# Solving the last slots of a fused matmul and decayed scan in halves of time, with shared PSUM banks for their transposes

## The chip, the cores and the metric

The kernel runs on one core of a Trainium2 chip. The metric is the time of one execution on the device in microseconds (us), the median of three timed runs. A profile of one further execution gives the span from its first to its last instruction, and each engine's instructions within it. TensorE is called PE, VectorE DVE, ScalarE ACT, GpSimd POOL, and SP is the engine that issues the stores.

## The reference

```python
B, S, D = (16, 2048, 1024)
xw = x @ w                       # x: B x S x D, w: D x D
out[:, 0, :] = xw[:, 0, :]
for t in range(1, S):
    out[:, t, :] = decay[None, :] * out[:, t - 1, :] + xw[:, t, :]
```

Each of the 1024 output channels is a first-order recurrence over time, run separately in each of 16 batches. All arrays are float32.

## The kernel before

**Tiling.** The 16 x 2048 time steps are cut into 64 chunks of 512. Input is loaded as bfloat16 with time on the partitions, transposed on DVE and copied by ACT into tiles `xt`, which hold input channels on the partitions and time along the free axis. The output channels are cut into K = 8 groups `n` of 128. A slot is one group of chunks (two chunks, or one chunk in the last two) with one `n`. For a slot, PE sums eight matmuls of 128 x 128 weights per chunk in a PSUM bank of 512 float32 columns: 128 output channels on the partitions, time along the free axis.

**Recurrence.** DVE runs it along the free axis with one scan instruction, in one of two ways. In an unpaired slot one scan (`run`, line 233) reads the PSUM bank and writes the solved tile `so`. In a paired slot ACT copies the bank to `xs` (`copy`, line 186) and scales its even columns (`odd`, line 169), POOL adds them to the odd columns (`join`, line 208), DVE scans half as many columns with the squared decay (`scan`, line 213), and then ACT scales (`even`) and POOL adds (`fill`, line 260) to recover the even columns. A tile takes the last column of the chunk before it as initial value.

**Output.** For almost all slots DVE transposes `so` in blocks of 32 x 32 into a tile `ot` (line 272), and SP stores it when four slots have filled it (line 296). The last four slots, called -4 to -1 here (R = 4; groups n = 4 to 7 of the last chunk), go another way: PE transposes each 128 x 128 block of `so` into PSUM against an identity matrix (line 398, `cross`), a copy brings the blocks of the four slots for the same 128 time steps to SBUF (line 416, `leave`), and SP stores them as 128 rows of 512 float32, which is 256 KB (line 418). The index `i` from 0 to 3 names the block of 128 time steps, and `r` from 0 to 3 names the slot: r = 0 is slot -4, r = 3 is slot -1.

**Order.** The order of instructions on each engine is that of the program. It is written by hand for the first and last slots, in the table `agenda`: a letter is an operation, the number after it the slot. `S` scans, `a` and `b` scan the first and second half of time, `h` and `c` complete a paired slot (ACT, then POOL), `R` and `V` are the functions `wedge` and `ending`. The last lines are:

```python
-3: "p-4 A-6 g-4 A-5 Z-7 Z-6 Z-5 j-4",
-2: "S-3 S-4",
-1: "a-2 h-4 c-4 a-1 R b-2 b-1 V",
```

Slot -4 is paired; slots -3, -2 and -1 are not. The matmuls of a slot are issued before its line of the table is performed. Slots -4, -3 and -2 are matmuls of 512 columns. Slot -1 alone is in halves of 256 columns, each half in a bank of its own (lines 625 to 633): eight matmuls of half 0, the transposes of slot -3 for blocks 0 and 1, six matmuls of half 1, then in `wedge` three transposes of block 0 and the last two matmuls. In `ending` the copy and store of block 0 come first, then three transposes of block 1, its copy and store, six transposes of blocks 2 and 3, and the last two (slot -1's) once its second half is scanned. Each of the four blocks has a PSUM bank and an SBUF tile of its own. ACT copies blocks 0 to 2, DVE copies block 3.

**PSUM.** There are eight banks: a ring `ps` of three tiles with room for two banks each, and one bank each named `spare` and `spare1`. `spare1` holds the squared decay, which paired scans read, until slot -4 has been scanned.

Of the kernel before, what the change touches and what calls it, by code (L numbers as in the profile page):

```python
# [14 lines left out]
def _ap(ap_obj: bass.AP, new_ap, extra_offset=0):  # L15
    return dataclasses.replace(
        ap_obj,
        ap=[list(p) for p in new_ap],
        offset=ap_obj.offset + extra_offset,
    )  # L20
# [5 lines left out]
def kernel(  # L26
# [26 lines left out]
    nc = tc.nc  # L53
    pin = tc.keep_in_program_order
    B, S, D = x.shape
    assert w.shape == (D, D)

    NQ = 4
    P = 32
    CQ = D // NQ  # L60
    K = CQ // P
    M = K // 2
    TL = 512
    NJ = TL // P
    NC = S // TL
    R = K // 2
    CH = D // 2
# [3 lines left out]
    sb = ctx.enter_context(tc.tile_pool(name="sb", bufs=1))  # L71
    psp = ctx.enter_context(tc.tile_pool(name="psp", bufs=1, space=bass.MemoryType.PSUM))
# [3 lines left out]
    def ring(pool, name, count, shape, dtype=FP32):  # L76
        i = turns[name] = turns.get(name, -1) + 1
        return pool.tile(shape, dtype, name=f"{name}{i % count}")
# [4 lines left out]
    chunks = [(b, c * TL) for b in range(B) for c in range(NC)]  # L83
    nch = len(chunks)
# [14 lines left out]
    xt_of = {}  # L99
# [25 lines left out]
    def matmul(ps, n, k, xt, t0=0, t1=TL, start=0, pairs=None):  # L125
        if pairs is None:
            rhs = xt[:, k // 2, k % 2, t0:t1]
        else:
            rhs = pairs[:, k // 2, t0 // P:t1 // P, :, k % 2].rearrange("p j i -> p (j i)")
        lhs = wsb[:, k, n].rearrange("p q i -> p (q i)")  # L130
        pin(nc.tensor.matmul(  # L131
            out=ps[:, t0:t1] if ps.shape[1] >= t1 else ps,
            lhsT=lhs,
            rhs=rhs,
            start=(k == 0 and t0 == start),
            stop=(k == K - 1),
        ))
# [3 lines left out]
    class Tile:  # L141
# [39 lines left out]
        def copy(self):  # L181
            self.xs = sb.tile([128, 2 * TL], FP32, name=f"xs{self.lot % 3}")[:, 0:self.T]
            parts = self.ps if isinstance(self.ps, tuple) else (self.ps,)
            size = self.T // len(parts)
            for i, ps in enumerate(parts):
                pin(nc.scalar.copy(out=self.xs[:, i * size:(i + 1) * size], in_=ps))  # L186
# [55 lines left out]
        def scan_half(self, half):  # L242
# [2 lines left out]
            ps = self.ps[half] if isinstance(self.ps, tuple) else self.ps[:, t:t + size]  # L245
            self.run(ps, t, size)

        def complete(self):
            if self.paired:
                self.even()  # L250
                self.fill()
            if self.keep is not None:
                self.save()
# [51 lines left out]
    size = M * CH  # L305
# [18 lines left out]
    spare = ring(psp, "spare", 1, [128, TL])  # L324
# [18 lines left out]
    for q in range(NQ):  # L343
        pin(nc.sync.dma_start(
            out=rows[q * P:q * P + R],
# [40 lines left out]
            out=ident, in_=ident, compare_op=ALU.not_equal, fill=1.0, base=0,  # L386
            pattern=[[-1, 128]], channel_multiplier=1))

    blocks = []

    def bank(name, count):
        return ring(psp, name, count, [128, R, 128])

    def cross(rs, some):
        for i in some:
            for r in rs:
                t = 2 + i * 128
                pin(nc.tensor.transpose(  # L398
                    out=blocks[i][:, r], in_=tiles[len(slots) - R + r].so[:, t:t + 128], identity=ident))

    def advance(count):
        for half, k, t in ends[:count]:
            matmul(half, K - 1, k, xt_of[nch - 1], t, t + TL // 2, t)
        del ends[:count]

    def wedge(i):
        cross((2, R - 1, 0), (0,))
        advance(2)

    def ending(i):  # L410
        b, t0 = chunks[-1]
        wides = [ring(sb, *spot, [128, NQ, R, P])
                 for spot in (("xb", 3), ("xb", 3), ("xb", 3), ("h", 4))]

        def leave(i, copy):
            pin(copy(out=wides[i].rearrange("p q r i -> p r q i"),  # L416
                     in_=blocks[i].rearrange("p r (q i) -> p r q i", q=NQ)))
            pin(nc.sync.dma_start(
                out=_ap(out, [[D, 128], [1, CH]], (b * S + t0 + i * 128) * D + CH),
                in_=wides[i].rearrange("p q r i -> p (q r i)")))  # L420

        leave(0, nc.scalar.copy)
        cross((2, 0, R - 1), (1,))
        leave(1, nc.scalar.copy)
        blocks.extend(bank(name, count) for name, count in (("ps", 3), ("spare", 1)))
        cross((1, 0, 2), (2, 3))
        cross((R - 1,), (2, 3))
        leave(2, nc.scalar.copy)
        leave(3, nc.vector.tensor_copy)

    slots = [(g, n) for g in groups[:-1] for n in range(K)]
    slots += [([c], n) for c in groups[-1] for n in range(K)]
    tiles = []

    def turn_and_load(c):
# [24 lines left out]
        "d": square_again,  # L460
        "I": identity,
        "V": ending,
        "R": wedge,
        "p": lambda s: tiles[s % len(slots)].copy(),
        "g": lambda s: tiles[s % len(slots)].odd(),
        "z": lambda s: tiles[s % len(slots)].zero(),
# [66 lines left out]
    }  # L533
    flips = (1, 13, 15, -19, -18, -11, -8, -6, -3, -2)
    later = {}
# [35 lines left out]
    for step, (g, n) in enumerate(slots):  # L571
        T = TL * len(g)
        left = step - len(slots)
        if n % R == 0:
            ns, nj = range(n, n + R), T // P
            if left == -2 * R:
                outlets = [Outlet(ns, H, half) for half in range(2)]
            else:
                pieces = 1 if left < -7 * R else 2 if left < -6 * R else nj // H
                outlets = [Outlet(ns, nj, pieces=pieces)]  # L580
        if left == -R:
            outlets = []
        if step == 0:
            heads = [ring(psp, "ps", 3, [128, T]) for _ in range(3)]
            firsts = [ps[:, 0:TL] for ps in heads] + [spares[0]]
            seconds = [ps[:, TL:T] for ps in heads] + [spares[1]]
            for j0, j1 in halves:
                for k in range(0, K, 2):
                    for i in range(R):
                        matmul(firsts[i], i, k, xt_of[0], j0 * P, j1 * P, pairs=xw_of[0])  # L590
            for k in range(1, K, 2):
                for i in range(R):
                    matmul(firsts[i], i, k, xt_of[0])
            for k0 in range(0, K, 2):
                for i in range(R):
                    for k in (k0, k0 + 1):
                        matmul(seconds[i], i, k, xt_of[1], 0, H * P,
                               pairs=xw_of[1] if k0 < 4 else None)
            for i in range(R):
                for k in range(K):  # L600
                    matmul(seconds[i], i, k, xt_of[1], H * P, TL, H * P,
                           pairs=xw_of[1] if i < 2 else None)
        if step < R:
            ps = heads[n] if n < 3 else tuple(spares)
        else:
            if step == K + 1:
                ps = nexts
            elif len(g) == 2 or n % R < 3:
                ps = ring(psp, "ps", 3, [128, T])
            else:  # L610
                ps = ring(psp, "spare", 1, [128, TL])
            todo = [(k, l) for k in range(K) for l in range(len(g))]
            if step < K:
                todo.sort(key=lambda kl: kl[0] % 2)
            elif step == K:
                todo = []
                nexts = (ring(psp, "spare", 1, [128, TL]), ring(psp, "ps", 3, [128, TL]))
                for l in range(len(g)):
                    for i, half in enumerate((ps[:, l * TL:(l + 1) * TL], nexts[l])):
                        for k in range(K):  # L620
                            matmul(half, n + i, k, xt_of.get(g[l]),
                                   pairs=xw_of[g[l]] if g[l] in (3,) else None)
            elif step == K + 1:
                todo = []
            if left == -1:
                ps = tuple(both[:, t:t + TL // 2] for t, both in zip(
                    (0, TL // 2), (ps, ring(psp, "ps", 3, [128, TL]))))
                blocks += [bank("spare1", 1), bank("ps", 3)]
                ends = [(half, k, t) for t, half in zip((0, TL // 2), ps) for k in range(K)]
                advance(K)  # L630
                cross((1,), (0, 1))
                advance(K - 2)
                todo = []
            if 40 <= step < 190:
                pin(nc.tensor.nop(hint="x", nofuse=True))
            for k, l in todo:
                matmul(ps[:, l * TL:(l + 1) * TL], n, k, xt_of[g[l]])
        tiles.append(Tile(g, n, ps, outlets))
        do = agenda.get(step, agenda.get(left) if left >= -20 else None)
        if do is None:  # L640
            do = usual(step)
        else:
            do = do.split()
            if left == -20:
                do = rest(step) + do
        perform(do)
# [29 lines left out]
```

## Time and profile before

| what | value |
|---|---|
| median of three timed runs | 904.1 us (904.0, 904.1, 904.33) |
| span of the profiled execution | 902.5 us |
| median less that span | 1.6 us |
| mean granted PE clock | 0.999 |
| instructions | 12285 |
| first matmul of slot -4 | 889.40 |
| matmuls of slot -1, first half | 894.58 to 895.62 |
| last matmul | ends 897.11 |
| last PE transpose | ends 898.39 |
| last copy | ends 899.12 |
| four last stores issued | 897.54, 898.09, 898.93, 899.36 |
| data of these stores on the DMA engines | 898.40 to 901.13 |

The lower rows are from the timeline of the profiled execution, in us from the span's start. A matmul's row covers its fill and drain, so the rows of neighbouring matmuls overlap; the distance of their starts is what each costs in a stream. A row such as `L131 PE MATMUL ps<-xt,wsb 128*128 128x512 bf16 x24` gives line, engine, operation, output and inputs, shapes, and how many neighbours were merged into it. At its end, in brackets, stands the idle time of the engine before it and what ended it.

### The profile page before, as it was taken

What the parts mean: (1) busy time and instruction counts of PE and PEld (TensorE: products, weight loads), DVE (VectorE), ACT (ScalarE), POOL (GpSimd) and SP (SyncE); (2) the same over time, 40 slices, a digit from 0 to 9 for tenths busy, and PEclk for the clock granted to TensorE, in tenths of its full rate; (3) what the DMA queues carried; (4) which work ended last, traced back from release to release, by engine and by line L of the source; (5) the groups of instructions that cost most, each with busy time, mean ns of one, the idle gap of its engine ahead of it and who ended that gap; (6) DMA issues with size and microseconds to landing.
All of it is one profiled execution on the core that took longest, in us unless ns stands there. A gap on an engine that the chain in (4) does not pass through costs nothing.

```text
span 902.5 us, 12285 instructions
## 1 busy us (share of the span) xinstructions
PE 896.7 (99%) x4201; PEld 411.4 (46%) x4201; DVE 824.2 (91%) x632; ACT 686.9 (76%) x958; POOL 656.6 (73%) x755
## 2 busy tenths in 40 slices
PE   9999999999999999999999999999999999999998
PEld 5544444444444444444444444444444444444444
DVE  4999998998999999999998999999999999999998
ACT  4889867777877877878778778777787787787743
POOL 7888678777767768777677687777777776876632
PEclk9999999999999999999999999999999999999999
DMA  9999999999999999999999999999999999999858
GB/s 193 194 215 220 231 231 206 215 231 243 251 249 248 242 251 246 244 250 253 227 236 228 221 228 230 232 227 227 232 230 228 227 234 223 228 226 218 183 142 236
DMA packets 403182, 204.77 MB, mean 227 GB/s; under 512 B 9392, under 2 KB 402096, under 8 KB 403120
## 3 DMA queue, kind: packets, MB, share of 16 engines
q1 hardware_dynamic: 265808, 134.77, 60.8%
q0 software_dynamic: 137024, 68.70, 56.8%
q8 instruction: 33, 0.54, 0.2%
q10 hardware_dynamic: 288, 0.52, 0.2%
q14 instruction: 29, 0.24, 0.1%
HBM read 138.42 MB, written 134.22 MB: 302 GB/s over the span
## 4 chain that ended last, share of the span: by engine, by line
PE 98%; DMA 1%; POOL 0%; issue 0%; DVE 0%; DVEq 0%; POOLq 0%
PE ps L131 96%; PE spare L131 1%; DMA xb<-in_x_dram 1%; DMA ot<-in_w_dram 1%; POOL ot L313 0%; PE spare L398 0%; PE ps L398 0%; DVE h L416 0%; DVE wsb L320 0%; DVEq L320 0%; POOLq L660 0%
## 5 line engine op out<-in xcount | busy, mean ns | idle before, releaser
L131 PE MATMUL ps<-xt,wsb 128*128 128x512 bf16 x4016 | 866.1, 378 | 0.5 <-DVE wsb L320 0.5
L131 PEld LDWEIGHTS <-wsb 128*128 128x128 bf16 x4152 | 405.9, 98 | 479.7 <-ACT wsb L320 0.8
L208 POOL TENSOR_TENSOR xs<-h,xs 128x512 f32<-128x512 f32 (+1 forms) x190 | 242.5, 1276 | 187.1 <-ACT h L169 85.5
L186 ACT COPY xs<-ps 128x1024 f32<-128x1024 f32 (+1 forms) x190 | 188.9, 994 | 152.8 <-PE ps L131 147.7
L272 DVE STREAM_TRANSPOSE ot<-so 128x1024 f32<-128x1024 f32 (+2 forms) x264 | 300.1, 1175 | 4.5 <-DMA out_dram<-ot 2.3
L260 POOL TENSOR_TENSOR so<-h,xs 128x512 f32<-128x512 f32 (+1 forms) x190 | 241.1, 1271 | 45.2 <-ACT h L169 28.0
L123 ACT COPY xt<-xw 128x2048 bf16<-128x2048 bf16 (+1 forms) x136 | 242.2, 1789 | 7.8 <-DVE xw L115 7.8
L105 POOL DMA_DIRECT2D xb<-in_x_dram x264 | 174.0, 660 | 3.5 <-DMA ot<-in_w_dram 1.1
L169 ACT ACTIVATE h<-so,dec 128x512 f32<-128x512 f32 (+1 forms) x190 | 145.4, 766 | 29.8 <-DVE so L213 26.7
L115 DVE STREAM_TRANSPOSE xw<-xb 128x2048 f32<-128x2048 f32 (+1 forms) x78 | 147.3, 1900 | 7.0 <-DMA xb<-in_x_dram 7.0
L213 DVE TENSOR_TENSOR_SCAN so<-spare,keep,xs 128x512 f32<-128x512 f32 (+1 forms) x97 | 119.8, 1237 | 25.7 <-POOL xs L208 25.4
L213 DVE TENSOR_TENSOR_SCAN so<-spare,xs 128x512 f32<-128x512 f32 x93 | 113.1, 1218 | 26.5 <-POOL xs L208 23.6
L169 ACT ACTIVATE h<-ps,dec 128x512 f32<-128x512 f32 (+1 forms) x189 | 129.4, 685 | 0.0
L233 DVE TENSOR_TENSOR_SCAN so<-dec,ps 128x1024 f32<-128x1024 f32 x34 | 76.7, 2259 | 1.0 <-ACT h L169 1.0
L233 DVE TENSOR_TENSOR_SCAN so<-dec,keep,ps 128x1024 f32<-128x1024 f32 (+2 forms) x35 | 75.4, 2153 | 0.0
L264 ACT COPY keep<-so 128x1 f32<-128x1 f32 x136 | 25.2, 188 | 9.4 <-DVE so L233 9.0
L204 ACT COPY so<-keep 128x1 f32<-128x1 f32 x97 | 18.5, 192 | 2.7 <-DVE ot L272 2.5
L131 PE MATMUL spare<-xt,wsb 128*128 128x512 bf16 (+1 forms) x56 | 11.9, 341 | 0.0
L131 PE MATMUL ps<-xw,wsb 128*128 128x256 bf16 (+1 forms) x68 | 11.2, 301 | 0.0
L202 POOL MEMSET so<- 128x1 f32 x93 | 10.6, 116 | 0.6 <-DVE ot L272 0.6
L313 POOL DMA_DIRECT2D ot<-in_w_dram x12 | 6.5, 544 | 3.2 <-DMA xb<-in_x_dram 2.1
L338 PE MATMUL spare<-idle 128*128 128x512 bf16 x22 | 7.5, 519 | 1.2 <-DVE idle L328 1.2
(39 smaller groups left out, 39.3 us busy)
## 6 DMA issues: line engine op xcount, KB each, us to landing
out_dram<-ot SPq DMA_DIRECT2D x236, 512.0 KB, 10.9
xb<-in_x_dram POOLq DMA_DIRECT2D x248, 256.0 KB, 7.9
out_dram<-ot SPq DMA_DIRECT2D x56, 128.0 KB, 2.6
xb<-in_x_dram POOLq DMA_DIRECT2D x16, 128.0 KB, 5.8
out_dram<-ot SPq DMA_DIRECT2D x8, 256.0 KB, 4.2
ot<-in_w_dram POOLq DMA_DIRECT2D x12, 128.0 KB, 5.1
out_dram<-xb SPq DMA_DIRECT2D x3, 256.0 KB
ot<-in_w_dram ACTq DMA_DIRECT2D x2, 256.0 KB, 5.1
```

What stands on the lines that cost most here:

```text
L105: pin(nc.gpsimd.dma_start(out=xb_of[c][quad(q), j0:j1], in_=_ap(x, [[D, P], [P * D, j1 - j0], [1, CQ]], (b * S + t0 + j0 * P) * D + q * CQ)))
L115: pin(nc.vector.transpose(out=dst.rearrange("p (m j i) -> p j m i", m=M, i=P)[:, j0:j1, m0:m1], in_=src.rearrange("p (j m c) -> p j m c", ...
L123: pin(copy(out=xt_of[c][:, m0:m1, :, j0 * P:j1 * P], in_=src))
L131: pin(nc.tensor.matmul(out=ps[:, t0:t1] if ps.shape[1] >= t1 else ps, lhsT=lhs, rhs=rhs, start=(k == 0 and t0 == start), stop=(k == K - 1),))
L169: pin(nc.scalar.activation(out=h, in_=src, func=mybir.ActivationFunctionType.Copy, scale=dec[:, self.n:self.n + 1]))
L186: pin(nc.scalar.copy(out=self.xs[:, i * size:(i + 1) * size], in_=ps))
L208: pin(nc.gpsimd.tensor_tensor(out=odds, in0=self.g, in1=odds, op=ALU.add))
L213: pin(nc.vector.tensor_tensor_scan(out=so[:, 3:T + 2:2], data0=squares[-1][:, n:n + 1].to_broadcast([128, T // 2]), data1=self.xs[:, 1:T:2 ...
L233: pin(nc.vector.tensor_tensor_scan(out=so[:, t + 2:t + 2 + size], data0=dec[:, n:n + 1].to_broadcast([128, size]), data1=ps, initial=befor ...
L260: pin(nc.gpsimd.tensor_tensor(out=self.so[:, 2:T + 2:2], in0=self.h, in1=self.xs[:, 0:T:2], op=ALU.add))
L264: pin(nc.scalar.copy(out=self.keep, in_=self.so[:, self.T + 1:self.T + 2]))
L272: pin(nc.vector.transpose(out=outlet.ot[:, :, c0:c0 + P], in_=self.so[:, 2 + t0:2 + t0 + nj * P].rearrange("p (i t) -> p i t", t=P)))
```

## The change

The change touches only the last four slots and the functions that write them out.

Slot -2's matmuls are split into halves of 256 columns like those of slot -1. PE now issues: slots -4 and -3 whole, half 0 of -2, half 0 of -1, half 1 of -2, eight transposes (blocks 0 and 1 of all four slots), half 1 of -1, eight transposes (blocks 2 and 3). Slot -3's matmuls stay whole, but its scan is split into halves (`a-3`, `b-3`). Slot -4's scan moves ahead of that of slot -3. The second half of the last scan goes in two pieces of 128 columns (`e-1`, `f-1`).

The tiles of the ring `ps` for slots -4 to -2 take two banks each (`tops`). The transposes go into four banks by pairs of blocks and pairs of slots: blocks 0 and 1 of slots -4 and -3 share one bank, blocks 0 and 1 of slots -2 and -1 the next, and blocks 2 and 3 likewise share the two banks in which the matmuls of slots -4 and -3 had been. Slot -2's halves lie in the two banks of the third tile; slot -1's halves lie in `spare` and `spare1`.

The copies go piece by piece (`carry`): ACT copies 512, 256 and 256 columns for blocks 0 and 1; then ACT copies 512 columns (slots -4 and -3 of blocks 2 and 3), DVE copies 256 (slots -2 and -1 of block 2), and ACT copies twice 128 (slot -2, then slot -1, of block 3). All blocks go through one SBUF tile. The four stores stay as they were, of 256 KB each from SP.

```diff
+        def scan_part(self, t, size):
+            half = self.T // 2
+            ps = self.ps[t // half] if isinstance(self.ps, tuple) else self.ps
+            t0 = t % half if isinstance(self.ps, tuple) else t
+            self.run(ps[:, t0:t0 + size], t, size)
...
     def cross(rs, some):
-        for i in some:
-            for r in rs:
+        for r in rs:
+            for i in some:
                 t = 2 + i * 128
                 pin(nc.tensor.transpose(
-                    out=blocks[i][:, r], in_=tiles[len(slots) - R + r].so[:, t:t + 128], identity=ident))
...
+                    out=banks[i // 2 * 2 + r // 2][:, i % 2, :, r % 2],
+                    in_=tiles[len(slots) - R + r].so[:, t:t + 128], identity=ident))
+
+    def carry(copy, i0, i1, r0, r1):
+        src = banks[i0 // 2 * 2 + r0 // 2][:, i0 % 2:i0 % 2 + i1 - i0, :, r0 % 2:r0 % 2 + r1 - r0]
+        dst = wides[0][:, i0:i1, :, r0:r1]
...
+    def half_slot(s, half):
+        tile_ = tiles[s % len(slots)]
+        t = half * TL // 2
+        for k in range(K):
+            matmul(tile_.ps[half], tile_.n, k, xt_of[nch - 1], t, t + TL // 2, t)
 
     def ending(i):
...
+        wides.append(ring(sb, "xb", 3, [128, NQ, NQ, R, P]))
+        cross((1, 0, 2, 3), (0, 1))
+        half_slot(-1, 1)
+        carry(nc.scalar.copy, 0, 2, 0, 2)
+        carry(nc.scalar.copy, 0, 1, 2, 4)
+        leave(nc.sync, 0)
+        carry(nc.scalar.copy, 1, 2, 2, 4)
+        leave(nc.sync, 1)
+
+    def closing(i):
+        cross((0, 1, 2), (2, 3))
+        cross((3,), (2,))
+        cross((3,), (3,))
+        carry(nc.scalar.copy, 2, 4, 0, 2)
+        carry(nc.vector.tensor_copy, 2, 3, 2, 4)
+        leave(nc.sync, 2)
+        carry(nc.scalar.copy, 3, 4, 2, 3)
+        carry(nc.scalar.copy, 3, 4, 3, 4)
+        leave(nc.sync, 3)
...
+        "e": lambda s: tiles[s % len(slots)].scan_part(TL // 2, TL // 4),
+        "f": lambda s: tiles[s % len(slots)].scan_part(TL * 3 // 4, TL // 4),
...
-        -2: "S-3 S-4",
-        -1: "a-2 h-4 c-4 a-1 R b-2 b-1 V",
+        -2: "S-4 a-3 h-4 c-4 a-2",
+        -1: "a-1 V b-3 b-2 e-1 f-1 R",
...
+            elif -R <= left < -1:
+                tops.append(ring(psp, "ps", 3, [128, 2 * TL]))
+                ps = tops[-1][:, 0:TL]
+                if left == -2:
+                    ps = (tops[-1][:, 0:TL // 2], tops[-1][:, TL:TL * 3 // 2])
...
+        if left >= -2:
+            half_slot(left, 0)
+        if left == -1:
+            half_slot(-2, 1)
+            banks += [both[:, t:t + TL].rearrange("p (b q r i) -> p b q r i", b=2, q=NQ, r=2)
+                      for t, both in ((TL, tops[0]), (TL, tops[1]), (0, tops[0]), (0, tops[1]))]
```

More of the change, by code (lines that the diff above doesn't have):

```diff
@@ L387, in identity @@
             pattern=[[-1, 128]], channel_multiplier=1))
-    blocks = []
-    def bank(name, count):
-        return ring(psp, name, count, [128, R, 128])
+    tops = []
+    banks = []
+    wides = []
     def cross(rs, some):
-        for i in some:
-            for r in rs:
+        for r in rs:
+            for i in some:
                 t = 2 + i * 128
                 pin(nc.tensor.transpose(
-                    out=blocks[i][:, r], in_=tiles[len(slots) - R + r].so[:, t:t + 128], identity=ident))
@@ L401, in advance @@
[L401 to L408, printed above, removed]
-    def ending(i):
[L411 to L429, printed above, removed]
+                    out=banks[i // 2 * 2 + r // 2][:, i % 2, :, r % 2],
@@ new lines, in cross @@
+                    in_=tiles[len(slots) - R + r].so[:, t:t + 128], identity=ident))
+    def carry(copy, i0, i1, r0, r1):
+        src = banks[i0 // 2 * 2 + r0 // 2][:, i0 % 2:i0 % 2 + i1 - i0, :, r0 % 2:r0 % 2 + r1 - r0]
+        dst = wides[0][:, i0:i1, :, r0:r1]
+        if r1 - r0 == 2:
+            pin(copy(out=dst.rearrange("p b q r i -> p b q (r i)"),
+                     in_=src.rearrange("p b q r i -> p b q (r i)")))
+        else:
+            pin(copy(out=dst[:, :, :, 0], in_=src[:, :, :, 0]))
@@ new lines, in leave @@
+    def leave(queue, i):
+        b, t0 = chunks[-1]
+        pin(queue.dma_start(
+            out=_ap(out, [[D, 128], [1, CH]], (b * S + t0 + i * 128) * D + CH),
+            in_=wides[0][:, i].rearrange("p q r i -> p (q r i)")))
+    def half_slot(s, half):
[3 more added lines that the diff above has]
+            matmul(tile_.ps[half], tile_.n, k, xt_of[nch - 1], t, t + TL // 2, t)
+    def ending(i):
+        wides.append(ring(sb, "xb", 3, [128, NQ, NQ, R, P]))
[6 more added lines that the diff above has]
+        leave(nc.sync, 1)
@@ L462 @@
         "V": ending,
-        "R": wedge,
+        "R": closing,
+        "e": lambda s: tiles[s % len(slots)].scan_part(TL // 2, TL // 4),
+        "f": lambda s: tiles[s % len(slots)].scan_part(TL * 3 // 4, TL // 4),
         "p": lambda s: tiles[s % len(slots)].copy(),
@@ L607 @@
                 ps = nexts
+            elif -R <= left < -1:
[3 more added lines that the diff above has]
+                    ps = (tops[-1][:, 0:TL // 2], tops[-1][:, TL:TL * 3 // 2])
             elif len(g) == 2 or n % R < 3:
                 ps = ring(psp, "ps", 3, [128, T])
+            elif left == -1:
+                ps = (ring(psp, "spare", 1, [128, TL])[:, 0:TL // 2],
+                      ring(psp, "spare1", 1, [128, TL])[:, 0:TL // 2])
             else:
@@ L624 @@
                 todo = []
[L625 to L632, printed above, removed]
+            if left >= -2:
                 todo = []
@@ L638 @@
         tiles.append(Tile(g, n, ps, outlets))
+        if left >= -2:
+            half_slot(left, 0)
[3 more added lines that the diff above has]
+                      for t, both in ((TL, tops[0]), (TL, tops[1]), (0, tops[0]), (0, tops[1]))]
         do = agenda.get(step, agenda.get(left) if left >= -20 else None)
```

## The prediction

> **What bounds the kernel now.** I read the engines' busy shares first, then the chain of work that ended last, then the last 12 us in order of time, and last the DMA share in short stretches.
>
> ```profile
> PE 896.7 (99%) x4201; PEld 411.4 (46%) x4201; DVE 824.2 (91%) x632; ACT 686.9 (76%) x958; POOL 656.6 (73%) x755
> ...
> PE 98%; DMA 1%; POOL 0%; issue 0%; DVE 0%; DVEq 0%; POOLq 0%
> ```
>
> TensorE (PE) is busy for 99% of the span, and 98% of the chain is PE. The diff leaves every slot up to -4 as it is and issues the same columns of matmul (a slot of 512 becomes two halves), so about 889 us of the span can't move. What can move is what lies behind the matmuls of slot -4.
>
> ```profile
> 889.40 5.34 PE L131 MATMUL ps<-xt,wsb 128*128 128x512 bf16 x24
> ...
> 892.43 0.73 POOL L208 TENSOR_TENSOR xs<-h,xs 128x256 f32<-128x256 f32 x1 [2.19 <-ACT h L169]
> 893.11 1.28 DVE L233 TENSOR_TENSOR_SCAN so<-dec,keep,ps 128x512 f32<-128x512 f32 x1
> 894.30 0.73 DVE L213 TENSOR_TENSOR_SCAN so<-spare,keep,xs 128x256 f32<-128x256 f32 x1
> 894.58 1.04 PE L131 MATMUL spare<-xt,wsb 128*128 128x256 bf16 x8
> ...
> 896.32 1.58 DVE L233 TENSOR_TENSOR_SCAN so<-dec,so,ps 128x256 f32<-128x256 f32 x2
> ...
> 896.73 0.38 PE L131 MATMUL ps<-xt,wsb 128*128 128x256 bf16 x2
> ...
> 898.12 0.27 PE L398 MATMUL spare<-ident,so 128*128 128x128 f32 x1
> ...
> 898.43 0.69 DVE L416 COPY h<-spare 128x512 f32<-128x512 f32 x1 [0.53 <-PE spare L398]
> 899.36 0.40 SPq L418 DMA_DIRECT2D out_dram<-h  x1
> ```
>
> The columns are start, duration, engine, line and operation. Slots -4 to -2 are the 24 matmuls from 889.40 (0.216 us each). Slot -1 is in halves (0.109 each); its last matmul ends at 897.11. The last scan b-1 starts 0.06 later, the last transpose ends at 898.39, the last copy at 899.12. Four stores of 256 KB are issued at 897.54, 898.09, 898.93 and 899.36. The stretches show what ends last:
>
> ```profile
> 897.90:898.40 0.50, 0.49 (x4) 0.20 (x2) 0.00 (x0) 0.24 (x2) 0.00 (x0) 1.00 0.02 5
> 898.40:899.09 0.69, 0.00 (x0) 0.00 (x0) 0.66 (x1) 0.50 (x1) 0.00 (x0) 1.00 1.02 380
> 899.09:899.78 0.69, 0.00 (x0) 0.00 (x0) 0.03 (x1) 0.00 (x0) 0.00 (x0) 1.00 1.00 365
> 899.78:900.47 0.69, 0.00 (x0) 0.00 (x0) 0.00 (x0) 0.00 (x0) 0.00 (x0) 1.00 1.03 380
> 900.47:901.13 0.66, 0.00 (x0) 0.00 (x0) 0.00 (x0) 0.00 (x0) 0.00 (x0) 0.64 1.04 400
> 901.30:902.50 1.20, 0.00 (x0) 0.00 (x0) 0.00 (x0) 0.00 (x0) 0.00 (x0) 0.50 0.00 0
> ```
>
> The last two columns are the DMA engines' share and GB/s. The older stores are through by 897.9; from 898.40 the four stores fill all 16 engines, 0.69 us each, with no gap. So **the end is bound by the stores' data**: first packet 0.86 us behind the first issue (897.54 to 898.40), four times 0.69, and about 1.3 us of closing. The third store could start at 898.93 + 0.86 = 899.79, just when the second is through: issue and data are level there.
>
> **The change, part by part.** Times are on this execution's clock; its span is 902.5, the median of the three timed runs 904.1, so 1.6 us lie around the span and I carry them over.
>
> *DVE order.* S-4 moves ahead of slot -3's scan. It waits for the POOL add that ends at 893.16, so it starts at 893.2 instead of 894.30. The 512 scan becomes two of 256: a 256 follows the next after 0.66 (894.30 to 894.95), so two take 1.32 against 1.19 (893.11 to 894.30), +0.13. Then a-3 starts at 893.86, a-2 at 894.51, a-1 at 895.17 (ends 895.90), b-3 at 895.83, b-2 at 896.49 (ends 897.22). The matmuls each needs are done before.
>
> *Pair completion.* In the trace h-4 (ACT) starts 0.03 behind S-4's end and c-4 (POOL) ends 1.34 behind h-4's start (895.06 to 896.40). So c-4 ends near 895.3 instead of 896.40.
>
> *PE order.* Halves -2a, -1a, -2b take 3 x 0.87 from 892.85 to 895.45, then eight transposes of 0.11 to 896.33, then half -1b to 897.20, with its last matmul ending at 897.36. The transposes find a-3, c-4 (needed at 895.67, cover 0.37), a-2 and a-1 (needed at 896.11, cover 0.2) done; without that cover each microsecond of lateness costs one, because half -1b is queued behind them. Before, five transposes stood ahead of that end; now eight do: **the last matmul ends 0.25 later**.
>
> *Last scan in two.* No row shows a 128 scan. 512 takes 1.255, 256 takes 0.73; the line gives 0.46, the next start 0.40 on. Bounds are 0.17 (the DVE's 128x8 copy) and 0.73; I take the line, since 256 is near. e-1 runs from 897.42 to 897.88, f-1 from 897.82 to 898.28. The last transpose then starts at 898.33 and ends at 898.60, 0.21 later than before. The split wins nothing for that one (unsplit, the scan would end at 898.15 and the two transposes at 898.58); it only brings block 2's transpose forward, to 897.93.
>
> *First two stores.* Bank pair 0 is complete at 896.05, pair 1 at 896.49. An ACT copy of 512 takes 0.585; 256 I take at 0.37 (bounds 0.19, the one-element copy, and 0.585; the 0.48 of the strided activation lies between). The copies end near 897.0 and 897.35; the stores go out at 897.03 and 897.46 (SP's issues follow at 0.43: 898.93 to 899.36), about 0.5 and 0.6 earlier. First packet 897.93, where the older stores end; both are through at 899.31.
>
> *Last two stores.* Row blocks 2 and 3 of slots -2 and -1 now share one PSUM bank, and the DVE copy of block 2 stands in program order behind the transpose that writes block 3 there. No row of before has one engine reading a bank that PE still writes: there each bank is handed on whole (transposes end 896.89, copy starts 896.93). I take it that this stays so, and the copy waits for the last transpose: 898.64. A DVE copy of 512 takes 0.69; 256 I take at 0.42 (bounds 0.17 and 0.69). It ends at 899.06, the store goes out at 899.09 instead of 898.93, its first packet comes at 899.95. The DMA engines have then been idle since 899.31. The last two ACT copies (128 elements, 0.27 each by the same line, bounds 0.19 and 0.585) run beside or, if ACT must also wait for DVE on the bank, behind it and end at 899.1 or 899.6; the last store goes out by 899.6, ready at 900.46, before the third is through at 900.64. The end of data is 899.95 + 0.69 + 0.66 = 901.30 against 901.13.
>
> **Sum: +0.17 us**, span 902.7, time 904.3. The 0.5 us gained at the first two stores is not on the path any more: the queue runs dry and the third store sets the end. The other edits (8 more weight loads of about 0.1 beside matmuls of 0.109, as in half -1a now; no ring slot reused early; the earlier stores' issues untouched) cost nothing in this cover; if the loads were not hidden, 0.1 us each would be late.
>
> The Trainium skill, page "PSUM — Partial Sum Buffer", section "PSUM bank collisions raise a hardware error", says that two engines may not use one bank and quadrant at once, whatever the columns, so accesses need guarding by bank. That speaks against copying a shared bank piecewise, and by it the sum is the +0.17; the trace of before can't show it, as it has no such pair of accesses. The page "DMA: Bandwidth & Descriptors", section "Latency and other measured facts", gives about 0.6 us to the first byte of a store issued from SP. The 0.86 here differs from it, and the measurement decides; by 0.6 the third store would start at 899.69 and the sum would be -0.09.
>
> **The rivals.**
> 1. *The pieces do run early.* The DVE copy waits only for its own transpose (starts at 897.93, ends at 898.2) and for f-1 on its queue: it runs from 898.3 to 898.72, store three at 898.75, packets from 899.61; the last ACT copy runs from 898.64 to 898.91, store four at 899.18 (SP's 0.43), and its data ends at 900.99. That is -0.14: 904.0. For it: one SBUF tile is read in pieces by ACT (10.20) while DVE still writes other pieces (to 11.14). Against: no such row in PSUM.
> 2. *Slower: the two-bank tiles are waited for whole.* Slot -2's halves now lie in two banks of one tile. If the matmuls of -2b must wait for a-2, which reads the other half (ends 895.23), PE starts them 0.69 late; and if b-3 waits for the transposes into its tile's other bank (then ending near 897.2), b-2, e-1 and f-1 follow in line: f-1 ends at 899.4, the DVE copy at 900.2, store three has packets at 901.1 and the data ends at 902.45, +1.3: 905.4. It decides as soon as a wait covers more than a bank. Against it stand the SBUF rows of rival 1; no row of before shows it in PSUM.
> 3. *Slower: the shared output tile.* All four blocks now go through one SBUF tile. If each copy waited for the store of the block before to land (897.54 to about 899.6, 2.05 us, at the first store now), store two would go out at 899.4, three at 902.1, four at 904.6, and the data would end near 906.2: +5, 909. Before, each block had its own tile. Against: the pieces of xw above, written and read side by side.
> 4. *The order does not hold:* c-4 or a-1 is late at the transposes. Covers are 0.37 and 0.2; beyond them the price is one to one. Being 0.5 late gives 904.6.
>
> **How the numbers follow.** Forecast (shared bank waited for) 0.64, 904.3; rival 1 0.22, 904.0; rival 4 0.06, 904.6; rival 2 0.05, 905.4; rival 3 0.03, 909. The bounds on the unshown sizes move the forecast: a 128 scan as short as 0.17 makes the end of data 0.36 earlier (903.9), one as long as 0.73 makes it 0.5 later (904.8); the copy's bounds add about 0.25 either way. The range is 903.7 to 904.9. A measurement of this kernel tells about 0.2% (1.8 us) from no change; within it lie all cases but rival 3 and accidents of the kind of rivals 2 and 4. So faster 0.02, within 0.93, slower 0.05.
>
> **What would show it.** In the changed kernel: S-4 at 893.2; eight transposes in a row from 895.45 with no gap; the last matmul ending near 897.36; two scans of 0.46; the first store issued near 897.0; a gap of some 0.6 us in the DMA share near 899.3 to 899.95; the DVE copy starting behind the last transpose. I am wrong if that copy starts before it, if the DMA gap is missing, or if PE idles ahead of -2b or -1b.

## The result and the profile after

The changed kernel takes 906.39 us (8 runs, 906.15 to 906.78) where the kernel before takes 904.22 (8 runs beside it): the ratio is 1.0025, with a 95% interval of 1.0016 to 1.0034. It is slower by about 2.2 us, outside the range of 903.7 to 904.9. The profiled execution has a span of 904.8 us against 902.5. Its page, as the one of before was read, with busy time by engine and then the chain that ended last:

```profile
PE 892.1 (99%) x4127; PEld 411.9 (46%) x4209; DVE 824.9 (91%) x634; ACT 687.2 (76%) x961; POOL 656.7 (73%) x755
...
PE 97%; DMA 1%; issue 1%; DVE 0%; POOL 0%; ACT 0%; ACTq 0%; DVEq 0%; POOLq 0%
```

(Some of PE's records are missing in this trace: 4127 matmuls against 4209 weight loads.) The shares hardly move; the loss is a quarter of a per cent and lies in the last 10 us. Slot -4's first matmul starts at 889.46 here and at 889.40 before, so nothing ahead of it has changed. From there the timeline reads (start, duration, engine, line, operation; in brackets the idle time before and what ended it):

```profile
893.25 0.75 DVE L213 TENSOR_TENSOR_SCAN so<-spare,keep,xs 128x256 f32<-128x256 f32 x1
...
895.20 0.73 DVE L233 TENSOR_TENSOR_SCAN so<-dec,keep,spare 128x256 f32<-128x256 f32 x1
895.34 1.03 PE L131 MATMUL ps<-xt,wsb 128*128 128x256 bf16 x8 [0.52 <-DVE so L233]
896.21 1.04 PE L403 MATMUL ps<-ident,so 128*128 128x128 f32 x8
896.84 1.14 ACT L411 COPY xb<-ps 128x512 f32<-128x512 f32 x3 [2.27 <-PE ps L403]
897.08 1.04 PE L131 MATMUL spare<-xt,wsb 128*128 128x256 bf16 x8
897.73 4.28 SPq L418 DMA_DIRECT2D out_dram<-xb  x4
...
898.01 1.39 DVE L233 TENSOR_TENSOR_SCAN so<-dec,so,ps 128x256 f32<-128x256 f32 x2 [2.09 <-ACT xb L411]
...
899.31 0.97 DVE L233 TENSOR_TENSOR_SCAN so<-dec,so,spare 128x128 f32<-128x128 f32 x2
...
900.71 0.42 DVE L411 COPY xb<-ps 128x256 f32<-128x256 f32 x1 [0.42 <-PE ps L403]
901.17 0.43 ACT L414 COPY xb<-ps 128x128 f32<-128x128 f32 x2 [1.29 <-DVE xb L411]
```

Four waits are new. PE stands idle for 0.52 us ahead of the second half of slot -2 (-2b), until the scan a-2 has ended. DVE stands idle for 2.09 us behind a-1, until ACT's three copies of blocks 0 and 1 end at 897.98; then b-3 starts at once. The DVE copy of block 2 starts behind the last transpose (900.34 plus 0.33). And ACT's last copies start only when that DVE copy has ended. The last two waits are between users of one bank, and the forecast had them; the first two are between users of different banks of one tile, and it did not. The stretches of the DMA engines' data (last two columns: share, GB/s):

```profile
897.73:898.58 0.85, 0.60 (x6) 0.35 (x3) 0.57 (x1) 0.25 (x1) 0.00 (x0) 1.00 0.00 0
898.58:899.28 0.70, 0.44 (x2) 0.20 (x2) 0.70 (x2) 0.00 (x0) 0.00 (x0) 1.00 1.01 375
899.28:900.10 0.82, 0.55 (x3) 0.35 (x3) 0.78 (x3) 0.58 (x1) 0.00 (x0) 1.00 0.86 320
900.10:902.02 1.92, 0.39 (x2) 0.14 (x1) 0.61 (x2) 0.43 (x2) 0.00 (x0) 0.88 0.00 0
902.02:902.72 0.70, 0.00 (x0) 0.00 (x0) 0.00 (x0) 0.00 (x0) 0.00 (x0) 0.50 0.99 369
902.72:903.54 0.82, 0.00 (x0) 0.00 (x0) 0.00 (x0) 0.00 (x0) 0.00 (x0) 0.50 0.88 325
```

The first two stores are through at 900.10. The third is issued only at 901.20 and has its first packet at 902.02, so the queue is empty for 1.9 us; before, the four stores followed one another without a gap. SP's row of that third store:

```profile
901.20 0.33 SPq L418 DMA_DIRECT2D out_dram<-xb  x1
```

### The profile page after: what moved, and what is told of

It is laid out like the page before. It is cut to its first block, busy times and chain, and to the rows that moved or that the text cites. A ratio compares the mean times of both kernels' runs of the same rounds, so it can differ in the third digit from the quotient of the medians.

```text
span 904.8 us, 12223 instructions
## 1 busy us (share of the span) xinstructions
PE 892.1 (99%) x4127; PEld 411.9 (46%) x4209; DVE 824.9 (91%) x634; ACT 687.2 (76%) x961; POOL 656.7 (73%) x755
## 4 chain that ended last, share of the span: by engine, by line
PE 97%; DMA 1%; issue 1%; DVE 0%; POOL 0%; ACT 0%; ACTq 0%; DVEq 0%; POOLq 0%
PE ps L131 95%; PE spare L131 1%; DMA xb<-in_x_dram 1%; DMA ot<-in_w_dram 1%; DVE so L233 0%; POOL ot L319 0%; PE ps L403 0%; POOL xs L208 0%; ACT xb L411 0%; ACT xs L186 0%; DVE xb L411 0%; ACT h L169 0%; DVE wsb L326 0%; ACT xb L414 0%; ACTq L698 0%
```

## The experiments

**Theory T:** a tile in PSUM is waited for whole. An instruction waits for what another engine did earlier in program order on any part of the same tile, in another bank too, and also where both only read. **Rival B:** waits go by bank, as the forecast had it; then b-3's wait must come from something else (two engines reading PSUM at once, a late input), and the idle PE from the halves themselves.

Starts of the runs differ by up to a microsecond, so beside each time stands the *tail*: from the start of slot -4's first matmul to the end of the span of the profiled execution. It is 13.12 before (902.52 less 889.40) and 15.34 after (904.80 less 889.46).

| kernel | time, us | ratio to before, 95% interval | tail, us |
|---|---|---|---|
| before | 904.22 | 1 | 13.12 |
| after | 906.39 | 1.0025 (1.0016 to 1.0034) | 15.34 |
| 1: scans first | 905.27 | 1.0014 (1.0005 to 1.0023) | 14.32 |
| 2: slot -2 whole | 905.88 | 1.0021 (1.0012 to 1.0030) | 15.01 |
| 3: banks swapped | 906.03 | 1.0021 (1.0012 to 1.0030) | 14.79 |
| 4: before, one tile | 904.95 | 1.0009 (1.0000 to 1.0018) | 14.00 |
| 5: tiles apart | 904.32 | 1.0000 (0.9991 to 1.0009) | 13.04 |
| 6: apart, by block | 904.40 | 1.0001 (0.9992 to 1.0010) | 13.18 |
| 7: before, two readers | 904.52 | 1.0002 (0.9993 to 1.0011) | 13.28 |

The kernel before took 904.06 beside 1 to 4 and 904.36 beside 5 to 7. The intervals are about 0.8 us to either side. So the times tell the changed kernel and experiments 1 to 3 from the kernel before (experiment 4 barely), but not 1 to 3 from the changed kernel; what is said of those rests on the rows and the tail, from one profiled execution each.

### 1. The scans ahead of the transposes

```diff
-        -1: "a-1 V b-3 b-2 e-1 f-1 R",
+        -1: "a-1 b-3 b-2 V e-1 f-1 R",
```

> Edit: in the changed kernel the scans b-3 and b-2 stand ahead of the first eight transposes and their copies in program order; the order on each engine stays the same. Theory T (a PSUM tile is waited for whole: an instruction waits for what any other engine did earlier in program order on any part of the tile, the reads of it too): b-3 no longer comes after ACT's reads of its tile, so it follows a-1 directly at about 895.9 instead of 898.01, b-2 follows at 896.5, e-1 at about 898.2 behind the last matmul; the third store goes out near 899.9 instead of 901.16. Span 1.3 us less than the changed kernel, time about 905.1. Rival B (waits go by bank, and b-3 stands still because ACT and DVE read PSUM at the same time, or because DVE lacked something else that came late): b-3 still starts near 898.0, time 906.4.

The order on each engine is the same as in the changed kernel; only which instruction counts as earlier differs. The timeline of this kernel (slot -4 starts at 889.17):

```profile
894.92 0.72 DVE L233 TENSOR_TENSOR_SCAN so<-dec,keep,spare 128x256 f32<-128x256 f32 x1
895.05 1.03 PE L131 MATMUL ps<-xt,wsb 128*128 128x256 bf16 x8 [0.52 <-DVE so L233]
895.56 1.36 DVE L233 TENSOR_TENSOR_SCAN so<-dec,so,ps 128x256 f32<-128x256 f32 x2
895.92 1.07 PE L403 MATMUL ps<-ident,so 128*128 128x128 f32 x8
896.56 1.14 ACT L411 COPY xb<-ps 128x512 f32<-128x512 f32 x3 [2.27 <-PE ps L403]
```

b-3 now starts at 895.56, 0.64 behind a-1's start and with no idle time, and the tail is 1.02 us shorter. So b-3's 2.09 us were no lack of data. ACT's copies run from 896.56 with b-2 (until 896.92) on DVE beside them, so the wait was not for two engines reading PSUM at once either. This is as T has it. The gain is 0.3 less than expected, about half of it because e-1 and f-1 take 0.99 together and not 0.86.

### 2. Slot -2 whole

```diff
-                if left == -2:
-                    ps = (tops[-1][:, 0:TL // 2], tops[-1][:, TL:TL * 3 // 2])
...
-        if left >= -2:
-            half_slot(left, 0)
-        if left == -1:
-            half_slot(-2, 1)
+        if left == -1:
+            half_slot(-1, 0)
```

> Edit: slot -2's matmuls are whole again (eight of 512 columns into one bank of its own tile), all else of the change stays. Theory T: the idle time of 0.52 us on PE ahead of the second half of slot -2 goes, since no second half has to wait for a-2, which reads the other bank of that tile; but a-1 is then the last to be ready for the transposes (about 896.4), so half 1 of slot -1 starts only 0.36 earlier, the copies end about 0.3 earlier, and b-3, still waiting for them, starts near 897.7. Span 0.3 less than the changed kernel, time about 906.1. Rival B (the idle time is the price of having the halves at all, and b-3 waits for something else): PE has no such idle time, but b-3 does not move with the copies: time 906.4.

The timeline (slot -4 starts at 889.11):

```profile
896.17 0.44 PE L403 MATMUL ps<-ident,so 128*128 128x128 f32 x2 [0.18 <-DVE so L233]
...
896.65 0.65 ACT L411 COPY xb<-ps 128x256 f32<-128x256 f32 x2 [0.26 <-PE ps L403]
...
897.33 1.38 DVE L233 TENSOR_TENSOR_SCAN so<-dec,so,ps 128x256 f32<-128x256 f32 x2 [1.21 <-ACT xb L411]
```

The idle time ahead of -2b is gone; PE waits 0.18 for a-1 instead. The copies end at 897.30 and b-3 starts 0.03 later: it moves with them. The tail is 0.33 shorter, as T expected (0.3).

### 3. The two banks of blocks 0 and 1 swapped

```diff
-                      for t, both in ((TL, tops[0]), (TL, tops[1]), (0, tops[0]), (0, tops[1]))]
+                      for t, both in ((TL, tops[1]), (TL, tops[0]), (0, tops[0]), (0, tops[1]))]
```

> Edit: the two banks for the transposes of blocks 0 and 1 change places: those of slots -4 and -3 go into the second bank of slot -3's tile, those of slots -2 and -1 into the second bank of slot -4's tile. Nothing else changes; every bank is used as before. Theory T: b-3 reads slot -3's tile, in which ACT now reads only its first copy, which ends near 897.42; so b-3 starts near 897.46 instead of 898.01, everything behind it 0.55 earlier: span 904.2, time 905.85. Rival B (waits by bank, b-3 held by the ACT copies as such or by something else): b-3 stays at 898.0, time 906.4.

The two banks change places with all their users. The bank that b-3 reads keeps its own; only its neighbour in the tile is another. The timeline (slot -4 starts at 889.06):

```profile
896.45 1.14 ACT L411 COPY xb<-ps 128x512 f32<-128x512 f32 x3 [2.27 <-PE ps L403]
896.69 1.04 PE L131 MATMUL spare<-xt,wsb 128*128 128x256 bf16 x8
897.07 1.38 DVE L233 TENSOR_TENSOR_SCAN so<-dec,so,ps 128x256 f32<-128x256 f32 x2 [1.54 <-ACT xb L411]
```

b-3 starts at 897.07, 0.03 after the end of the first copy (896.45, and 0.59 for its 512 columns), while ACT goes on with the other two until 897.59. So it waits for the one copy that reads its own tile, and not for ACT as such. The tail is 0.55 shorter, the number expected. This run speaks most plainly against B.

### 4. The kernel before with one tile for both halves of slot -1

```diff
-                ps = tuple(both[:, t:t + TL // 2] for t, both in zip(
-                    (0, TL // 2), (ps, ring(psp, "ps", 3, [128, TL]))))
+                both = ring(psp, "ps", 3, [128, 2 * TL])
+                ps = (both[:, 0:TL // 2], both[:, TL:TL * 3 // 2])
```

> Edit: the kernel before, with one thing changed: the two halves of slot -1 lie in the two banks of one PSUM tile instead of in banks of two tiles. Theory T: a-1 waits for the six matmuls of the second half that stand ahead of it in program order, though they write the other bank: it starts near 896.5 instead of 895.65; the transpose of slot -1, the last two matmuls and b-2, b-1 behind them follow 0.7 to 0.8 late. Time about 905.0. Rival B (waits by bank): nothing changes, a-1 at 895.65, time 904.2.

The timeline (slot -4 starts at 889.14), with a-1 of the kernel before (slot -4 at 889.40) first:

```profile
895.65 0.75 DVE L233 TENSOR_TENSOR_SCAN so<-dec,keep,spare 128x256 f32<-128x256 f32 x1
...
895.42 0.82 PE L131 MATMUL ps<-xt,wsb 128*128 128x256 bf16 x6
...
896.27 0.75 DVE L233 TENSOR_TENSOR_SCAN so<-dec,keep,ps 128x256 f32<-128x256 f32 x1 [0.86 <-PE ps L131]
896.93 1.58 DVE L233 TENSOR_TENSOR_SCAN so<-dec,so,ps 128x256 f32<-128x256 f32 x2
897.08 0.44 PE L398 MATMUL spare<-ident,so 128*128 128x128 f32 x2 [0.73 <-DVE so L233]
```

a-1 reads one bank and waits 0.86 us for six matmuls that write the other. One part of the change, sharing a tile, put alone into the kernel before, costs 0.88 us of tail.

### 5. The changed schedule with the tiles apart

```diff
                 if left == -2:
-                    ps = (tops[-1][:, 0:TL // 2], tops[-1][:, TL:TL * 3 // 2])
+                    ps = (tops[-1][:, 0:TL // 2],
+                          ring(psp, "spare1", 1, [128, TL])[:, 0:TL // 2])
...
-                      ring(psp, "spare1", 1, [128, TL])[:, 0:TL // 2])
+                      tops[2][:, TL:TL * 3 // 2])
...
     def closing(i):
+        low = ring(psp, "spare", 1, [128, TL])
+        late = ring(psp, "spare1", 1, [128, TL])
+        banks.extend((view(low, 0), view(tops[1], 0), view(low, 0), view(late, 0)))
...
+            banks += [view(tops[0], TL), view(tops[0], 0)] * 2
```

Here `banks` holds two entries for each block, one for slots -4 and -3 and one for slots -2 and -1, and `view` gives one bank of a tile in the layout of the transposes.

> Edit: the changed kernel with its schedule, its halves, pieces, copies and stores as they are, and only the places in PSUM changed, so that no instruction touches a tile on which another engine still has something to do: slot -2's halves lie in two tiles, the transposes of blocks 0 and 1 all go into slot -4's tile, those of block 2 and of block 3 of slots -2 and -1 go into two tiles. Theory T: no idle time on PE ahead of slot -2's second half, b-3 right behind a-1, the DVE copy of block 2 right behind the last scan, the third store near 898.9 when slot -4 starts at 889.40 as in the kernel before; all of the 2.2 us comes back: time 904.1, span 902.5. Rival (the halves, the split scans and the smaller pieces cost time by themselves, beyond the waits): the waits go but 0.7 us or more stays, time 904.9 or above.

The timeline (slot -4 starts at 889.35):

```profile
893.68 1.91 PE L131 MATMUL spare<-xt,wsb 128*128 128x256 bf16 x16
...
895.43 1.04 PE L409 MATMUL ps<-ident,so 128*128 128x128 f32 x8
895.74 0.72 DVE L233 TENSOR_TENSOR_SCAN so<-dec,so,ps 128x256 f32<-128x256 f32 x1
896.30 1.04 PE L131 MATMUL ps<-xt,wsb 128*128 128x256 bf16 x8
896.38 0.72 DVE L233 TENSOR_TENSOR_SCAN so<-dec,so,spare 128x256 f32<-128x256 f32 x1
896.50 1.14 ACT L417 COPY xb<-ps 128x512 f32<-128x512 f32 x3 [2.04 <-PE ps L409]
...
897.38 1.00 DVE L233 TENSOR_TENSOR_SCAN so<-dec,so,ps 128x128 f32<-128x128 f32 x2 [0.28 <-PE ps L131]
...
898.29 0.42 DVE L417 COPY xb<-ps 128x256 f32<-128x256 f32 x1
898.43 0.33 PE L409 MATMUL spare<-ident,so 128*128 128x128 f32 x1 [0.18 <-DVE so L233]
```

Half -1a and half -2b are one run of 16 matmuls, b-3 and b-2 follow a-1, and the copy of block 2 starts ahead of the last transpose. SP's row of the third store:

```profile
898.77 0.33 SPq L424 DMA_DIRECT2D out_dram<-xb  x1
```

The tail is 13.04: all 2.3 us are back, with the same instructions, pieces and order. The halves, the split scans and the smaller copies cost nothing that shows.

Two things limit this run. It also parts the pieces of blocks 2 and 3 that shared one bank, so the 2.3 us hold the third and fourth wait too: behind the last transpose (898.43 plus 0.33) the copy of block 2 would start about 0.5 us later than its 898.29. By that estimate some 1.8 us belong to the waits across banks. And one such wait is left: blocks 0 and 1 lie in the two banks of slot -4's tile, the first copy needs only the first four of the eight transposes, and it starts (896.50) when all eight have ended (896.47).

### 6. Tiles apart, copies by block, last scan unsplit

```diff
-        carry(nc.scalar.copy, 0, 2, 0, 2)
+        carry(nc.scalar.copy, 0, 1, 0, 2)
         carry(nc.scalar.copy, 0, 1, 2, 4)
         leave(nc.sync, 0)
+        carry(nc.scalar.copy, 1, 2, 0, 2)
         carry(nc.scalar.copy, 1, 2, 2, 4)
...
-        carry(nc.vector.tensor_copy, 2, 3, 2, 4)
+        carry(nc.scalar.copy, 2, 3, 2, 4)
         leave(nc.sync, 2)
-        carry(nc.scalar.copy, 3, 4, 2, 3)
-        carry(nc.scalar.copy, 3, 4, 3, 4)
+        carry(nc.vector.tensor_copy, 3, 4, 2, 4)
```

> Edit: as the kernel with the tiles apart, and the copies go block by block (256 columns at a time for blocks 0 and 1, so that the first store goes out earlier; ACT copies block 2 and DVE the last 256 columns of block 3), and the last scan is not split. Theory T: first store near 897.3 instead of 897.5, the third bound by ACT's copy near 898.9: time 904.0, span 902.3 to 902.5, which a measurement can't tell from the kernel before. Rival (as for the kernel with tiles apart): 904.9 or above.

The first store goes out 7.82 us behind slot -4's start (898.12 less 890.30) instead of 8.14 before, but the last 256 columns of block 2 are copied only at 899.49 (9.19 behind; 8.94 in experiment 5): their transpose waits for the scan, which now ends as a whole at 899.07.

```profile
898.32 0.75 DVE L233 TENSOR_TENSOR_SCAN so<-dec,so,ps 128x256 f32<-128x256 f32 x1 [0.28 <-PE ps L131]
...
899.12 0.33 PE L409 MATMUL ps<-ident,so 128*128 128x128 f32 x1 [0.19 <-DVE so L233]
...
899.49 0.37 ACT L417 COPY xb<-ps 128x256 f32<-128x256 f32 x1
```

So the third store, at 899.88, is no earlier: 9.58 behind slot -4's start, against 9.42 in experiment 5 and 9.53 before. Tail 13.18, ratio 1.0001: it can't be told from the kernel before, and neither it nor experiment 5 is shown to beat it.

### 7. The kernel before with two readers on one tile

```diff
-        blocks.extend(bank(name, count) for name, count in (("ps", 3), ("spare", 1)))
+        both = ring(psp, "ps", 3, [128, 2 * TL])
+        blocks.extend(both[:, t:t + TL].rearrange("p (r i) -> p r i", r=R) for t in (0, TL))
```

> Edit: the kernel before, with one thing changed: blocks 2 and 3 are transposed into the two banks of one tile instead of into two tiles; ACT still copies the one and DVE the other, and no byte is touched by both. Theory T with reads included: ACT's copy of block 2 waits for the last transpose (898.43 instead of 898.32) and DVE's copy of block 3 waits for ACT's copy to end (starts near 899.05 instead of 898.43); the last store goes out near 899.8, the data ends 0.15 later: time 904.3. Rival (only writes are waited for, two readers are not held apart): DVE's copy starts near 898.43, beside ACT's, time 904.2.

The timeline (slot -4 starts at 889.28), with ACT's copy of the kernel before first:

```profile
898.32 0.58 ACT L416 COPY xb<-ps 128x512 f32<-128x512 f32 x1 [0.26 <-PE ps L398]
...
898.31 0.58 ACT L416 COPY xb<-ps 128x512 f32<-128x512 f32 x1 [0.37 <-PE ps L398]
898.93 0.69 DVE L416 COPY h<-ps 128x512 f32<-128x512 f32 x1 [1.15 <-ACT xb L416]
```

In the kernel before, ACT's copy starts at 898.32 and DVE's at 898.43, side by side. Here DVE's starts 0.04 after ACT's has ended: two reads of different banks are held apart because the tile is one. The tail is 0.16 longer (0.15 was expected) and the time the same within its interval, so this verdict rests on the row.

## Why the prediction was wrong

**What held.** The bound (the stores' data behind the last copies) held. So did the copy of block 2 behind the last transpose, the transposes in a row, c-4 well ahead of need, 0.42 for DVE's copy of 256 columns, 0.37 for ACT's (experiment 6), and 0.82 to 0.86 from the start of a store's issue to its first packet (897.73 to 898.58, 901.20 to 902.02; before 897.54 to 898.40). On that last, the 0.6 us of the Trainium skill, page "DMA: Bandwidth & Descriptors", section "Latency and other measured facts", is too low for these stores if it is counted from the start of the issue, though the queue was empty. Rivals 1, 3 and 4 did not come: that copy did not run early, the second store went out 0.46 behind the first (898.19 and 897.73), and no transpose of blocks 0 and 1 waited for c-4 or a-1. Of the signs of being wrong one came: PE idles ahead of -2b.

**The step that failed** is the one that let each instruction start when its data were there and its *bank* was free: "Then a-3 starts at 893.86, a-2 at 894.51, a-1 at 895.17 (ends 895.90), b-3 at 895.83, b-2 at 896.49", and "halves -2a, -1a, -2b take 3 x 0.87 from 892.85 to 895.45". Waits go by tile. Experiment 3 shows it for b-3, experiment 4 for a half of a slot and matmuls into the other bank. What the waits did, in the changed kernel against that schedule, moved by 0.06 for its later start:

- -2b starts at 895.34 instead of 894.64: +0.70. Experiment 2, in which PE waits 0.18 for a-1 in its place, gains 0.33 at the end; the lateness reaches the end only by way of the copies.
- b-3 starts at 898.01 instead of 895.89: +2.12. Experiment 1 removes this wait and 1.02 of tail; what then stays late is -2b and the last block's copies.
- f-1 ends at 900.28 instead of 898.34, and the third store goes out at 901.20 instead of 899.15: +2.05. With the 0.17 of the forecast that is the 2.2 measured.

**The rival that came true.** Rival 2 named this mechanism and gave it 0.05 and 905.4. Its place was right and its price too small. It took -2b to be 0.69 late (0.70 measured), but let b-3 wait only for the transposes into its tile (ending near 897.2), not for ACT's *reads* of it, which end 0.8 later, at 897.98. With 0.8 more it would have given 906.2. The evidence weighed against it, SBUF rows in which ACT reads a tile while DVE writes other pieces, is about SBUF: there the pieces run side by side, in PSUM they do not.

**The split scan** was mis-sized by little: two scans of 128 columns take 0.97 to 1.00 together, not 0.86. The second reads the first one's last column, and in experiment 5 they start 0.5 apart.

**The gain at the first stores** did not come. The forecast had the first store at 897.03, or 897.09 moved by 0.06; it went out at 897.73, 0.6 later, because the copies started about 0.7 late, behind -2b. With the tiles apart it goes out at 897.39, which is 8.04 behind slot -4's start, against 7.63 forecast and 8.14 before: there the first copy waits for transposes into the other bank of its tile (experiment 5).

**On the page that spoke against the change:** the Trainium skill, page "PSUM — Partial Sum Buffer", section "PSUM bank collisions raise a hardware error", forbids two engines on one bank and quadrant, and says that accesses to different banks run clean. The waits of experiments 4 and 7 are between different banks, so that rule does not ask for them; they come with the kernel's tiles. Whether the chip would run b-3 beside a copy from the other bank of one tile, with no wait between them, is not shown; in experiment 3 b-3 runs (from 897.07) beside ACT's copies of another tile (until 897.59).

## What to carry to other kernels

In a program built like this one, list before placing two users in one PSUM tile which engine touches it last in program order, in any bank and whether it reads or writes: the next engine waits for that, so a tile of two banks is one resource, not two. Free banks are worth little to a second engine unless they are tiles of their own: the same schedule cost 2.3 us or nothing by the placing alone, some 1.8 of it (an estimate, experiment 5) by waits across banks. When a forecast rests on waits that no row shows, price the wide wait with reads included, and give it more than a token chance.

## What the runs showed that was not expected

In these programs reads of one PSUM tile by two engines are held apart even in different banks: 0.04 us from the end of ACT's copy to the start of DVE's in experiment 7, 0.03 from ACT's last copy to b-3 in the changed kernel. And the start of the tail moves from run to run: slot -4's first matmul lay between 889.06 and 890.30 us in the nine profiled executions, so a single span can't tell differences of a few tenths at the end; the tail leaves that scatter out.
